# The recurrence's products of an mLSTM block as plain float32 matmuls instead of three float32r matmuls each

## The chip, the cores and the metric

The kernel runs on one core of a Trainium2 chip. The metric is the device time of one launch in microseconds (us). The engines are named as in the profile: PE is TensorE's matmul side and PEld its weight loads, DVE is VectorE, ACT is ScalarE, POOL is GpSimd, SP is the engine whose queue issues nearly all DMAs.

## The reference

The block takes x (2048 tokens x 1024 features, float32). It normalises x, projects it to four groups of 1024 columns, runs a pooling mixer on one half and a bidirectional mLSTM on the other, multiplies each by SiLU of its own z, and sends both through one output projection, a residual and a second norm. The change lies in the mLSTM alone. It has 4 heads of 256 features and 16 chunks of 128 tokens, and one scan per direction. Cut to what matters:

```
def step(carry, xs):                      # one chunk, one direction
    s   = (qj @ kj.T) * exp(log_D - m_t)                     # scores, weighted
    num = s @ vj + inter_w * (qj @ C)                        # chunk's values + state
    den = sum(s) + inter_w * (qj @ n)
    h   = num / max(|den|, exp(-m_t))
    C_new = decay * C + (ws * kj).T @ vj                     # update of the state
    n_new = decay * n + sum(ws * kj)
```

n is carried as a column beside C: the values end with a column of ones and a pad, so v has 258 columns.

## The kernel before, in words

Everything is float32 in memory, and nearly all large products are made of three float32r matmuls. A float32r operand is a float32 number whose low part is dropped; the kernel splits each operand into a high part (a cast on ScalarE) and a low part (the number minus its high part, on VectorE or GpSimd) and adds high x high, high x low and low x high in PSUM. The headwise maps (L336), the scores (L830) and the transposes are plain float32 matmuls already.

The order of the stages: input projections (`proj`, L135), the mLSTM's inputs (keys, values, convolved queries, written to DRAM), the gates, z of the first heads, the pooling mixer, then z of the last heads beside the 15 backward updates of head 0 (`next_backward`), and then the recurrence. It runs 64 steps (4 heads x 16 chunks). Step s computes both directions of its chunk from stored states: the forward state `cf` is carried on, the backward states `cb` of a head were made in the iterations of the head before it. What each iteration issues, in the order of every engine, is the table `order` (L991 to L1001): a piece, and by how many iterations it lags behind its step. In the first 53 iterations PE, DVE, ACT and POOL take exactly this order (`tc.manual_schedule`); for SP, and for all engines but PE later, a scheduler sets it.

One iteration has on PE: the forward `update` (two products of 128x128 weights by 258 columns), four units of the output projection (`fill`; a unit is three float32r matmuls of 512 columns, `po`, L704), `scores` of the next step, the backward `update`, two transposes `py`, a last part of units (`fill_rest`, on the mean 0.7 of one), and `numerators` (two products of scores by values and up to four of weighted queries by states). Around these, every operand is split: keys (`kh`, `kl`), values (`vh`, `vl`), states (`sh`, `sl`), weighted queries (`cwh`, `cwl`), weighted scores (`ph`, `pl`). The result `num` has one PSUM tile; VectorE makes the denominators from it (`denominators`), ScalarE and VectorE the ratios (`ratio0`, `ratio1`), which are its last readers. The updates' PSUM tile `upd` is also single, and VectorE adds it to the decayed state.

Small tiles in two buffers (pool `tp`) carry the pieces from one iteration to the next: `cw` (weighted queries, made by GpSimd two iterations ahead of their step), `dd` (weighted scores). The loaded keys `kk` have two buffers.

Of the kernel before, what the change touches and what calls it, by code (L numbers as in the profile page):

```python
# [10 lines left out]
F32 = mybir.dt.float32  # L11
F32R = mybir.dt.float32r
# [38 lines left out]
def hymba_block(ctx, tc, xT, x, w_in, wpxT, pool_w, bqT, bkT, bvT, bv, w_g, b_g, par, edge, w_out, g_out, out):  # L51
# [27 lines left out]
    # gate products that the recurrences use, token-major: column r = (dir, step, head)  # L79
# [16 lines left out]
    # ------------------------------------------------------------------ input projections  # L96
# [26 lines left out]
    # from the last z blocks on, TensorE runs in the order of the program  # L123
# [15 lines left out]
    # the small operands of the headwise maps, read ahead  # L139
# [3 lines left out]
    def load_headwise(i):  # L143
# [4 lines left out]
        # the map of q and, beside it, the gates' weights of k, q and v  # L148
# [12 lines left out]
    # W_poolx times the group's mix: pooling commutes with the mix of the channels  # L161
# [88 lines left out]
        # the array's clock rises while the first loads run  # L250
# [38 lines left out]
    # ---- the mLSTM's inputs  # L289
    with pm:  # L290
# [30 lines left out]
        def headwise(i, b):  # L321
# [3 lines left out]
            for src, off, rhs, dst in ((c, 0, mws[i], kk_s), (mxs[i], 2 + b * BT, hw[i]["vw"], v_s)):  # L325
                # v's columns end with ones, whose product with the keys is the denominator, and a pad
# [85 lines left out]
    # ---- z of the mLSTM (first heads) beside the gates: columns of gacc are (i|f, dir, head)  # L412
    with ExitStack() as pz:
# [31 lines left out]
        # in the order (dir, step, head)  # L445
# [15 lines left out]
        # rows r, columns t  # L461
# [34 lines left out]
        flat = lambda t: t.rearrange("p a b c -> p (a b c)")  # noqa: E731  # L496
# [30 lines left out]
    # ---- the pooling mixer  # L527
# [43 lines left out]
    # ------------------------------------------------------------------ mLSTM  # L571
# [21 lines left out]

    def keys_low(t):
        t["kl"] = t["pool"].tile([P, HD], F32R, name="kl")
        nc.vector.scalar_tensor_tensor(t["kl"], in0=t["k"], scalar=ws_tok[:, t["r"]:t["r"] + 1],  # L596
                                       in1=t["kh"].bitcast(F32), op0=ALU.mult, op1=ALU.subtract)

    def values_high(t):
        t["vh"] = t["pool"].tile([P, E], F32R, name="vh")  # L600
        nc.scalar.copy(t["vh"], t["v"])  # L601

    def values_low(t, eng=nc.gpsimd):
        t["vl"] = t["pool"].tile([P, E], F32R, name="vl")
        eng.tensor_tensor(t["vl"], t["v"], t["vh"].bitcast(F32), op=ALU.subtract)  # L605
# [20 lines left out]
    # the state that chunk j - 1 receives from its right  # L626
# [14 lines left out]
    def next_backward():  # L641
        if firsts:
# [3 lines left out]
            if "kh" not in bkv[f]:  # L646
                split_kv(bkv[f])
            backward(*f)
            if firsts and firsts[0] in bkv:
                split_kv(bkv[firsts[0]])  # L650

    # ---- the output projection: units of three products, and chores that go between them
# [67 lines left out]
    def fillers():  # L720
        # the first and the last tiles go in pairs by halves of the columns, while the other half's weights come
# [9 lines left out]
        def ahead(i):  # L731
            # reads y of piece i when it can be had
# [46 lines left out]
    # ---- a step of the forward direction, in pieces that go to different engines  # L779
# [20 lines left out]
    def mask(a):  # L800
        # keys s (partitions) that a query t may see: s <= t forward, s >= t backward
# [4 lines left out]
    # c times the weights of the states, and its parts  # L806
# [5 lines left out]

    def weighed_high(a):
        a["cwh"] = tp.tile([P, 2, 2, P], F32R, name="cwh")
        nc.scalar.copy(a["cwh"][:, a["ds"]], a["cw"][:, a["ds"]])  # L815

    def weighed_low(a, eng):
        ds = a["ds"]
        a["cwl"] = tp.tile([P, 2, 2, P], F32R, name="cwl")
        eng.tensor_tensor(a["cwl"][:, ds], a["cw"][:, ds], a["cwh"][:, ds].bitcast(F32), op=ALU.subtract)  # L820
# [284 lines left out]
```

## Time and profile before

| | |
|---|---|
| median of 3 runs | 1572.82 us (1572.33 to 1577.58) |
| profiled execution, first to last instruction | 1570.6 us |
| PE busy over the span | 1477.8 us (94%) |
| DVE / ACT / POOL busy | 1034.2 (66%) / 650.6 (41%) / 624.6 us (40%) |
| granted TensorE clock, mean | 0.992 of full speed |
| DMA | 231.25 MB, mean 147 GB/s |

The profiled execution lies 2.2 us under the median. A matmul's busy time reaches beyond the start of the next one, since matmuls are pipelined: what a matmul costs in a stream is the distance from its start to the next start. The recurrence lies between 857 us (first scores) and 1481 us (last scores); its iterations 0 to 52 end near 1325 us. After it only the rest of the output projection runs.

### The profile page before, as it was taken

The page shows a single profiled execution, that of the slowest core. Times are in us where ns is not written, and L with a number is a line of the kernel's source. Part 1 is how long each engine was busy: PE and PEld are TensorE (multiplying, and loading weights), DVE is VectorE, ACT ScalarE, POOL GpSimd, SP SyncE. Part 2 cuts the span into 40 slices and gives each one's busy share as a digit, 9 for nine tenths or more (in the row PEclk, how much of TensorE's full clock was granted, in tenths as well). Part 3 has the DMA queues.
Part 4 walks back from the last instruction along what each step waited for, and adds up shares of the span by engine and source line. Part 5 has one row for each costly group of instructions (what it writes and reads, how often), then busy time and mean ns, then how long its engine had stood idle before and what let it go on. Part 6 is the DMA issues. An engine that isn't in the chain of part 4 may idle for free.

```text
span 1570.6 us, 23151 instructions
## 1 busy us (share of the span) xinstructions
PE 1477.8 (94%) x7801; PEld 1257.9 (80%) x7801; DVE 1034.2 (66%) x1993; ACT 650.6 (41%) x1516; POOL 624.6 (40%) x752
## 2 busy tenths in 40 slices
PE   8899999999999999999999888888888899899998
PEld 6689888878888888888887777777777777787886
DVE  8795445562134333434543999999999999766753
ACT  6245443442011110001234666666666666635431
POOL 6543333310000222221020777777767778443300
PEclk9999999999999999999999999999999999999999
DMA  6268766542111101111337776676676667754352
GB/s 218 73 201 242 184 182 177 167 143 77 55 54 54 54 16 52 54 54 54 101 108 226 235 200 185 203 207 189 193 208 192 187 202 239 203 181 154 119 163 81
DMA packets 251351, 231.25 MB, mean 147 GB/s; under 512 B 18400, under 2 KB 211168, under 8 KB 250208
## 3 DMA queue, kind: packets, MB, share of 16 engines
q1 hardware_dynamic: 236768, 215.08, 45.9%
q10 hardware_dynamic: 14464, 14.68, 3.0%
q8 instruction: 62, 1.02, 0.3%
q14 instruction: 57, 0.47, 0.1%
HBM read 149.81 MB, written 79.89 MB: 146 GB/s over the span
## 4 chain that ended last, share of the span: by engine, by line
PE 56%; DVE 22%; DMA 8%; POOL 6%; issue 5%; ACT 3%; SPq 1%; POOLq 0%; DVEq 0%; ACTq 0%
PE proj L135 40%; PE po L704 7%; PE hw L336 4%; DVE yt L936 3%; DVE rstd L907 2%; DVE vl L605 2%; DMA gw<-g_s 2%; DVE cb L622 1%; DMA ym_s<-yt 1%; DVE yt L931 1%; PE hw L185 1%; DVE sl L869 1%; POOL cwl L820 1%; DVE kl L596 1%; POOL cw L810 1%
## 5 line engine op out<-in xcount | busy, mean ns | idle before, releaser
L135 PE MATMUL proj<-uh,whi 128*128 128x512 f32 x1024 | 403.8, 395 | 4.6 <-DVE mx L204 3.6
L135 PE MATMUL proj<-ul,whi 128*128 128x512 f32 x1024 | 401.5, 392 | 1.5 <-DVE ul L218 1.5
L135 PE MATMUL proj<-uh,wlo 128*128 128x512 f32 x1024 | 401.8, 393 | 0.4 <-DVE wlo L94 0.4
L135 PEld LDWEIGHTS proj<-uh,whi 128*128 128x128 f32 x1024 | 193.7, 189 | 43.3 <-DVE mx L204 3.7
L135 PEld LDWEIGHTS proj<-uh,wlo 128*128 128x128 f32 x1024 | 193.4, 189 | 41.7 <-DVE wlo L94 0.8
L135 PEld LDWEIGHTS proj<-ul,whi 128*128 128x128 f32 x1024 | 193.6, 189 | 40.9 <-DVE ul L218 2.6
L704 PE MATMUL po<-woh,yh 128*128 128x512 f32 x512 | 205.7, 402 | 3.2 <-DVE o L707 1.8
L704 PE MATMUL po<-woh,yl 128*128 128x512 f32 x512 | 202.4, 395 | 2.3 <-DVE yl L94 2.3
L704 PE MATMUL po<-wol,yh 128*128 128x512 f32 x512 | 202.0, 395 | 1.2 <-DVE wol L94 1.2
L91 ACT CAST whi<-wl 128x1024 fp32r<-128x1024 f32 x31 | 32.6, 1052 | 228.7 <-PE proj L135 225.5
L704 PEld LDWEIGHTS po<-woh,yl 128*128 128x128 f32 x512 | 96.6, 189 | 25.2 <-DVE yl L94 3.1
L616 PE MATMUL upd<-vh,kh 128*128 128x258 f32 x240 | 72.6, 302 | 46.8 <-ACT vh L601 45.1
L704 PEld LDWEIGHTS po<-woh,yh 128*128 128x128 f32 x512 | 96.7, 189 | 22.3 <-DVE o L707 2.4
L704 PEld LDWEIGHTS po<-wol,yh 128*128 128x128 f32 x512 | 96.8, 189 | 19.2 <-DVE wol L94 1.5
L316 DVE SCALAR_TENSOR_TENSOR c<-mx,par_sb,c 128x512 f32<-128x512 f32 x128 | 103.4, 825 | 3.0
L543 DVE TENSOR_TENSOR ux<-proj,rnorm 128x512 f32<-128x512 f32 x32 | 22.1, 691 | 124.7 <-PE proj L135 124.7
L869 POOL TENSOR_TENSOR sl<-cb,sh 128x516 fp32r<-128x516 f32 x60 | 86.5, 1441 | 29.9 <-ACT sh L864 25.4
L810 POOL TENSOR_TENSOR cw<-cT,gw 128x512 f32<-128x512 f32 (+1 forms) x64 | 91.8, 1434 | 7.8 <-DMA gw<-g_s 5.7
L556 POOL TENSOR_TENSOR win<-ux 128x2063 f32<-128x2063 f32 x8 | 29.0, 3624 | 160.7 <-DVE ux L543 160.7
L820 POOL TENSOR_TENSOR cwl<-cw,cwh 128x512 fp32r<-128x512 f32 (+1 forms) x64 | 90.3, 1411 | 6.4 <-ACT cwh L815 4.9
L616 PEld LDWEIGHTS upd<-vh,kh 128*128 128x128 f32 x240 | 45.2, 188 | 55.9 <-ACT hh L884 51.5
L843 POOL TENSOR_TENSOR pl<-dd,ph 128x256 fp32r<-128x256 f32 x64 | 51.4, 804 | 87.4 <-ACT ph L839 87.4
(216 smaller groups left out, 3187.4 us busy)
## 6 DMA issues: line engine op xcount, KB each, us to landing
gw<-g_s SPq DMA_DIRECT2D x128, 128.0 KB, 4.4
v<-v_s SPq DMA_DIRECT2D x124, 129.0 KB, 3.4
kk<-kk_s SPq DMA_DIRECT2D x124, 128.0 KB, 3.6
wl<-in_w_in SPq DMA_DIRECT2D x23, 512.0 KB, 3.9
xt<-in_xT SPq DMA_DIRECT2D x32, 256.0 KB, 4.1
cT_s<-c SPq DMA_DIRECT2D x32, 256.0 KB, 3.6
kk_s<-tokst SPq DMA_DIRECT2D x32, 256.0 KB, 2.6
kkT_s<-kkTb SPq DMA_DIRECT2D x32, 256.0 KB, 4.1
```

The costliest lines, as they stand in the source:

```text
L91: nc.scalar.copy(hi, src)
L135: pe(nc.tensor.matmul(ps, lhsT=l[:, kt, :], rhs=r[:, kt, :], start=(kt == 0 and n == 0), stop=(kt == KT - 1 and n == 2)))
L316: nc.vector.scalar_tensor_tensor(c, in0=mx[:, b * BT + t:(b + 1) * BT + t], scalar=par_sb[:, i, t:t + 1], in1=c, op0=ALU.mult, op1=ALU.add)
L336: nc.tensor.matmul(ps[:, e, :], lhsT=src[:, o:o + P], rhs=rhs, start=True, stop=True)
L605: eng.tensor_tensor(t["vl"], t["v"], t["vh"].bitcast(F32), op=ALU.subtract)
L616: pe(nc.tensor.matmul(ps[:, m, :E], lhsT=t[l][:, ms], rhs=t[r_], start=(n == 0), stop=(n == 2)))
L704: pe(nc.tensor.matmul(ps, lhsT=l[:, kt, :], rhs=r, start=(kt == 0 and e == 0), stop=(kt == 7 and e == 2)))
L810: eng.tensor_tensor(a["cw"][:, ds], a["cT"][:, None].broadcast_to([P, nd, 2, P]), a["gw"][:, 1, ds, None, :].broadcast_to([P, nd, 2, P]), ...
L820: eng.tensor_tensor(a["cwl"][:, ds], a["cw"][:, ds], a["cwh"][:, ds].bitcast(F32), op=ALU.subtract)
L843: eng.tensor_tensor(a["pl"], a["dd"], a["ph"].bitcast(F32), op=ALU.subtract)
L869: eng.tensor_tensor(a["sl", d], a["state", d], a["sh", d].bitcast(F32), op=ALU.subtract)
L936: eng.tensor_tensor(yt, yt, a["sz"], op=ALU.mult)
```

## The change

All products of the updates and numerators become one plain float32 matmul each, straight on the tiles that the parts were made from: `kw` (keys times the state weights, written as float32), `v`, `dd`, `cw` and the states `cf` and `cb`. The pieces that made parts, and their places in `order`, are gone. `v` gets a third buffer. The output projection and the input projections keep their three float32r matmuls. (The diff also drops comments; cut to its core here.)

```
-        v = pool.tile([P, E], F32, name="v", bufs=2)
+        v = pool.tile([P, E], F32, name="v", bufs=3)
-    def keys_high(t):
-        t["kh"] = t["pool"].tile([P, HD], F32R, name="kh")
-        nc.scalar.activation(t["kh"], t["k"], AF.Copy, scale=ws_tok[:, t["r"]:t["r"] + 1])
...
-    def keys_low(t):
...
-    def values_high(t):
...
-    def values_low(t, eng=nc.gpsimd):
...
-    def split_kv(t):
-        for piece in (keys_high, keys_low, values_high, values_low):
-            piece(t)
+    def weigh_keys(t):
+        t["kw"] = t["pool"].tile([P, HD], F32, name="kw")
+        nc.scalar.activation(t["kw"], t["k"], AF.Copy, scale=ws_tok[:, t["r"]:t["r"] + 1])
     def update(t, prev, pool, name, bufs):
...
-            for n, (l, r_) in enumerate((("kh", "vh"), ("kh", "vl"), ("kl", "vh"))):
-                pe(nc.tensor.matmul(ps[:, m, :E], lhsT=t[l][:, ms], rhs=t[r_], start=(n == 0), stop=(n == 2)))
+            pe(nc.tensor.matmul(ps[:, m, :E], lhsT=t["kw"][:, ms], rhs=t["v"], start=True, stop=True))
...
-    def weighed_high(a):
...
-    def weighed_low(a, eng):
...
-    def scores_high(a):
...
-    def scores_low(a, eng):
...
     def numerators(a):
...
-            for n, (l, r) in enumerate(((ph, kv["vh"]), (ph, kv["vl"]), (pl, kv["vh"]))):
-                pe(nc.tensor.matmul(num[:, d, :E], lhsT=l[:, d, :], rhs=r, start=(n == 0),
-                                    stop=(n == 2 and d not in a["dirs"])))
+            pe(nc.tensor.matmul(num[:, d, :E], lhsT=a["dd"][:, d, :], rhs=a["kv"]["v"], start=True,
+                                stop=d not in a["dirs"]))
         for d in a["dirs"][::-1]:
-            sh, sl = a["sh", d], a["sl", d]
+            state = cb.pop((a["h"], a["j"])) if d else a["cf"]
             for m in range(2):
-                for n, (l, r) in enumerate((("cwh", sh), ("cwh", sl), ("cwl", sh))):
-                    pe(nc.tensor.matmul(num[:, d, :E], lhsT=a[l][:, d, m, :], rhs=r[:, m, :],
-                                        start=False, stop=(m == 1 and n == 2)))
+                pe(nc.tensor.matmul(num[:, d, :E], lhsT=a["cw"][:, d, m, :], rhs=state[:, m, :],
+                                    start=False, stop=(m == 1)))
...
-    def state_high(a, d):
...
-    def state_low(a, d, eng):
...
     order = (
-        ("store", 3, V), ("scores_low", 0, G), ("denominators_2", 1), ("state_high_0", 0), ("ratio_0", 1),
-        ("forward", 0), ("back_values_high", -1), ("state_low_0", 0, V), ("ratio_1", 1), ("normalise_1", 2),
...
+        ("store", 3, V), ("denominators_2", 1), ("ratio_0", 1),
+        ("forward", 0), ("ratio_1", 1), ("normalise_1", 2),
+        ("fill", 0), ("fill", 0), ("moments_0", 1), ("fill", 0),
+        ("mask", -2), ("fill", 0), ("moments_1", 1), ("keys", -2),
+        ("scores", -1), ("moments_2", 1), ("backward", 0), ("transposes", 2), ("moments_3", 1),
         ("exponentials", -1), ("weigh", -2, G), ("normalise_0", 1), ("weigh_scores", -1), ("fill_rest", 0),
...
+        ("numerators", 0), ("back_keys", -1), ("join", 2), ("denominators_0", 0),
+        ("skip", 1), ("denominators_1", 0),
     )
```

What this does to the order on three engines, in the recurrence. PE before, from the end of a backward update (`upd`) over the transposes (`py`) and a unit of the output projection (`po`) to the first product of scores by values (`num`):

```order
L616 MATMUL upd<-vl,kh 128x258
L616 MATMUL upd<-vh,kl 128x258
L920 MATMUL py<-ident,hh 128x128 x2
L704 MATMUL po<-woh_6572,yh 128x512
L704 MATMUL po<-wol_6573,yh 128x512
L704 MATMUL po<-woh_6572,yl 128x512
L850 MATMUL num<-vh,ph 128x258
L850 MATMUL num<-vl,ph 128x258
L850 MATMUL num<-vh,pl 128x258
```

and the same place in the changed kernel:

```order
L597 MATMUL upd<-v,kw 128x258 x2
L869 MATMUL py<-ident,hh 128x128 x2
L685 MATMUL po<-woh_6422,yh 128x512
L685 MATMUL po<-wol_6423,yh 128x512
L685 MATMUL po<-woh_6422,yl 128x512
L812 MATMUL num<-v,dd 128x258 x2
L817 MATMUL num<-cb,cw 128x258 x2
L817 MATMUL num<-cf,cw 128x258 x2
```

A product was three rows (high by high, high by low, low by high) and is one; x2 stands for two products. The places in the iteration are the same.

GpSimd before, one iteration from the mask of the gate weights (`gw`) on, with what each instruction waits for besides its own engine's order:

```order
L803 AFFINE_SELECT gw<-gw 128x128 [waits DMAHW5_49]
L803 AFFINE_SELECT gw<-gw 128x128
L902 TENSOR_TENSOR rstd<-rstd,mhalf 128x1 [waits DVE_49]
L810 TENSOR_TENSOR cw<-cT,gw 128x512 [waits DMAHW6_49,DMAHW2_49,Pool_49]
L843 TENSOR_TENSOR pl<-dd,ph 128x256 [waits Activation_49]
L869 TENSOR_TENSOR sl_9609<-cb,sh_9564 128x516 [waits PE_49]
L820 TENSOR_TENSOR cwl<-cw,cwh 128x512
```

and after:

```order
L784 AFFINE_SELECT gw<-gw 128x128 [waits DMAHW2_49,Activation_49]
L784 AFFINE_SELECT gw<-gw 128x128
L851 TENSOR_TENSOR rstd<-rstd,mhalf 128x1 [waits DVE_49,Activation_49]
L791 TENSOR_TENSOR cw<-cT,gw 128x512 [waits DMAHW5_49,PE_49,Pool_49]
L784 AFFINE_SELECT gw<-gw 128x128 [waits DMAHW4_49,Activation_49]
```

Three of GpSimd's pieces (`pl`, `sl`, `cwl`) are gone. The weighted queries `cw` now wait for PE: their buffer was last read by GpSimd's `cwl` and ScalarE, and is now read by the numerators two steps back. Behind this wait stand the next mask and the next power (`rstd`).

VectorE before, from the backward state's evacuation (`cb`) to the reciprocal of the denominators (`rn`):

```order
L622 SCALAR_TENSOR_TENSOR cb<-cb,dec_bc,upd 128x516
L596 SCALAR_TENSOR_TENSOR kl<-kk,ws_tok,kh 128x256
L907 SCALAR_TENSOR_TENSOR rstd<-mv,rstd 128x1
L835 TENSOR_TENSOR dd<-dd,sT 128x256
L94 TENSOR_TENSOR yl<-y,yh 128x256
L596 SCALAR_TENSOR_TENSOR kl<-kk,ws_tok,kh 128x256
L931 SCALAR_TENSOR_TENSOR yt<-py,par_sb,yt 128x128 x2
L875 TENSOR_TENSOR rn<-num,em_tok 128x2
L605 TENSOR_TENSOR vl<-v,vh 128x258
L877 SCALAR_TENSOR_TENSOR rn<-num,rn 128x2
L936 TENSOR_TENSOR yt<-yt,sz 128x256
L880 RECIPROCAL rn<-rn 128x2
```

and after:

```order
L603 SCALAR_TENSOR_TENSOR cb<-cb,dec_bc,upd 128x516
L856 SCALAR_TENSOR_TENSOR rstd<-mv,rstd 128x1
L807 TENSOR_TENSOR dd<-dd,sT 128x256
L94 TENSOR_TENSOR yl<-y,yh 128x256
L880 SCALAR_TENSOR_TENSOR yt<-py,par_sb,yt 128x128 x2
L824 TENSOR_TENSOR rn<-num,em_tok 128x2
L826 SCALAR_TENSOR_TENSOR rn<-num,rn 128x2
L885 TENSOR_TENSOR yt<-yt,sz 128x256
L829 RECIPROCAL rn<-rn 128x2
```

Here two `kl` and one `vl` are gone (a `vl` and an `sl` more lie outside this piece); the rest keeps its order.

## Rows read from the trace of the kernel before

**Rows 1.** The page's head: the span of the profiled execution.
```profile
span 1570.6 us, 23151 instructions
```
**Rows 2.** Stretches (from:to us): length, busy us of engines (instructions), clock, DMA.
```profile
core 0: us, PE busy (x) PEld busy (x) DVE busy (x) ACT busy (x) POOL busy (x), PEclk, DMA share, GB/s
720.00:860.00 140.00, 140.00 (x665) 117.79 (x664) 58.23 (x77) 35.79 (x67) 23.21 (x21) 1.00 0.41 127
860.00:1325.00 465.00, 404.45 (x2499) 353.54 (x2498) 455.39 (x1047) 304.83 (x778) 334.65 (x363) 1.00 0.70 203
1325.00:1481.00 156.00, 148.45 (x764) 124.73 (x763) 115.47 (x271) 82.39 (x214) 68.71 (x78) 0.98 0.58 176
```
**Rows 3.** VectorE groups, 860 to 1325 us: xcount | busy us, mean ns | idle before.
```profile
L936 DVE TENSOR_TENSOR yt<-yt,sz 128x256 f32<-128x256 f32 x50 | 64.4, 1288 | 0.0
L596 DVE SCALAR_TENSOR_TENSOR kl<-kk,ws_tok,kh 128x256 fp32r<-128x256 f32 x97 | 55.6, 573 | 0.0
...
L869 DVE TENSOR_TENSOR sl<-cf,sh 128x516 fp32r<-128x516 f32 x48 | 49.9, 1039 | 0.0
L605 DVE TENSOR_TENSOR vl<-v,vh 128x258 fp32r<-128x258 f32 x97 | 46.8, 482 | 0.0
L622 DVE SCALAR_TENSOR_TENSOR cf<-cf,dec_bc,upd 128x516 f32<-128x516 f32 x45 | 32.7, 726 | 0.0
...
L880 DVE RECIPROCAL rn<-rn 128x2 f32<-128x2 f32 x51 | 7.8, 152 | 0.1
```
**Rows 4.** ScalarE group of the first ratio, same stretch.
```profile
L884 ACT ACTIVATE hh<-num,rn 128x256 f32<-128x256 f32 x51 | 24.2, 474 | 96.1 <-DVE rn L880 95.9
```
**Rows 5.** TensorE groups, same stretch.
```profile
L704 PE MATMUL po<-woh,yl 128*128 128x512 f32 x245 | 96.3, 393 | 0.0
...
L616 PE MATMUL upd<-vh,kh 128*128 128x258 f32 x188 | 57.8, 307 | 46.8 <-ACT vh L601 45.1 <-ACT woh L91 1.0 <-DVE cb L622 0.4
...
L856 PE MATMUL num<-sh,cwh 128*128 128x258 f32 x194 | 55.0, 283 | 0.0
...
L850 PE MATMUL num<-vh,ph 128*128 128x258 f32 x104 | 32.0, 308 | 2.4 <-DVE hh L888 0.7
L830 PE MATMUL sT<-cT,kkT 128*128 128x128 f32 x208 | 31.6, 274 | 1.4 <-DVE dd L835 1.4
...
L920 PE MATMUL py<-ident,hh 128*128 128x128 f32 x100 | 19.6, 277 | 5.1 <-ACT hh L910 5.1
```
**Rows 6.** TensorE timeline near 304 us: start us, us, line, tile, form, xcount.
```profile
303.82 1.14 PE L336 MATMUL hw<-mw,c 128*128 128x144 f32 x8
304.80 1.14 PE L336 MATMUL hw<-vw,mx 128*128 128x144 f32 x8
305.78 0.60 PE L344 MATMUL hw<-ident,tokst 128*128 128x128 f32 x4
```
**Rows 7.** TensorE timeline of one iteration of the recurrence, from 1199 us.
```profile
1199.17 0.28 PE L850 MATMUL num<-vl,ph 128*128 128x258 f32 x1
...
1201.12 0.28 PE L856 MATMUL num<-sh,cwl 128*128 128x258 f32 x1
...
1202.54 0.40 PE L704 MATMUL po<-wol,yh 128*128 128x512 f32 x1
...
1204.82 0.39 PE L704 MATMUL po<-woh,yl 128*128 128x512 f32 x1
1205.05 0.60 PE L830 MATMUL sT<-cT,kkT 128*128 128x128 f32 x4
```
**Rows 8.** TensorE groups over the whole span: the first record of each split product.
```profile
L616 PE MATMUL upd<-vh,kh 128*128 128x258 f32 x240 | 72.6, 302 | 46.8 <-ACT vh L601 45.1 <-ACT woh L91 1.0 <-DVE cb L622 0.4
...
L856 PE MATMUL num<-sh,cwh 128*128 128x258 f32 x240 | 68.3, 285 | 0.0
...
L850 PE MATMUL num<-vh,ph 128*128 128x258 f32 x128 | 39.1, 306 | 3.0 <-DVE hh L888 1.4
```
**Rows 9.** GpSimd group of the weighted queries, 860 to 1325 us.
```profile
L810 POOL TENSOR_TENSOR cw<-cT,gw 128x512 f32<-128x512 f32 x46 | 70.3, 1528 | 0.0
```

More of the change, by code (lines that the diff above doesn't have):

```diff
@@ L645, in next_backward @@
             f = firsts.pop(0)
-            if "kh" not in bkv[f]:
-                split_kv(bkv[f])
+            if "kw" not in bkv[f]:
+                weigh_keys(bkv[f])
             backward(*f)
             if firsts and firsts[0] in bkv:
-                split_kv(bkv[firsts[0]])
+                weigh_keys(bkv[firsts[0]])
     weights, wo, chores = {}, {}, []
@@ L811, in weigh @@
                           a["gw"][:, 1, ds, None, :].broadcast_to([P, nd, 2, P]), op=ALU.mult)
-    def weighed_high(a):
-        a["cwh"] = tp.tile([P, 2, 2, P], F32R, name="cwh")
-        nc.scalar.copy(a["cwh"][:, a["ds"]], a["cw"][:, a["ds"]])
-    def weighed_low(a, eng):
-        ds = a["ds"]
-        a["cwl"] = tp.tile([P, 2, 2, P], F32R, name="cwl")
-        eng.tensor_tensor(a["cwl"][:, ds], a["cw"][:, ds], a["cwh"][:, ds].bitcast(F32), op=ALU.subtract)
     def exponentials(a):
@@ L991, in hymba_block @@
     order = (
-        ("store", 3, V), ("scores_low", 0, G), ("denominators_2", 1), ("state_high_0", 0), ("ratio_0", 1),
-        ("forward", 0), ("back_values_high", -1), ("state_low_0", 0, V), ("ratio_1", 1), ("normalise_1", 2),
-        ("fill", 0), ("fill", 0), ("state_low_1", 0, G), ("moments_0", 1), ("weighed_low", 0, G), ("fill", 0),
-        ("mask", -2), ("fill", 0), ("values_high", -1), ("moments_1", 1), ("keys_high", -2), ("values_low", -1, V),
-        ("scores", -1), ("moments_2", 1), ("backward", 0), ("transposes", 2), ("moments_3", 1), ("keys_low", -1),
+        ("store", 3, V), ("denominators_2", 1), ("ratio_0", 1),
@@ L997, in hymba_block @@
+        ("forward", 0), ("ratio_1", 1), ("normalise_1", 2),
+        ("fill", 0), ("fill", 0), ("moments_0", 1), ("fill", 0),
+        ("mask", -2), ("fill", 0), ("moments_1", 1), ("keys", -2),
+        ("scores", -1), ("moments_2", 1), ("backward", 0), ("transposes", 2), ("moments_3", 1),
         ("exponentials", -1), ("weigh", -2, G), ("normalise_0", 1), ("weigh_scores", -1), ("fill_rest", 0),
-        ("numerators", 0), ("back_keys_high", -1), ("back_keys_low", -1), ("join", 2), ("denominators_0", 0),
@@ L999, in hymba_block @@
-        ("back_values_low", -1, V), ("skip", 1), ("denominators_1", 0), ("weighed_high", -1), ("state_high_1", -1),
-        ("scores_high", -1),
+        ("numerators", 0), ("back_keys", -1), ("join", 2), ("denominators_0", 0),
+        ("skip", 1), ("denominators_1", 0),
     )
     pieces = dict(
-        keys_high=lambda t: keys_high(t["kv"]), keys_low=lambda t: keys_low(t["kv"]),
-        values_high=lambda t: values_high(t["kv"]), values_low=lambda t, e: values_low(t["kv"], e),
-        mask=mask, weigh=weigh, weighed_high=weighed_high, weighed_low=weighed_low, exponentials=exponentials,
@@ L1006, in hymba_block @@
-        scores=scores, weigh_scores=weigh_scores, scores_high=scores_high, scores_low=scores_low,
+        keys=lambda t: weigh_keys(t["kv"]),
+        mask=mask, weigh=weigh, exponentials=exponentials, scores=scores, weigh_scores=weigh_scores,
         numerators=numerators, ratio_0=ratio0, ratio_1=ratio1, forward=forward, skip=skip,
         transposes=transpose_step, join=join, store=store_step)
-    for n, piece in (("state_high", state_high), ("state_low", state_low), ("denominators", denominators),
-                     ("moments", moments), ("normalise", normalise)):
+    for n, piece in (("denominators", denominators), ("moments", moments), ("normalise", normalise)):
@@ L1011, in hymba_block @@
         pieces.update({f"{n}_{k}": lambda t, *e, k=k, piece=piece: piece(t, k, *e) for k in range(4)})
-    backs = dict(back_keys_high=keys_high, back_keys_low=keys_low, back_values_high=values_high,
-                 back_values_low=values_low)
+    backs = dict(back_keys=weigh_keys)
     def run(span):
```

19 lines of the change are left out of this document (removed).

## The prediction

> **What bounds the kernel now.** I read the stretches first, then the groups of VectorE and TensorE inside the one that stood out, then TensorE's timeline for the distance from start to start. The profiled execution lasts 1570.6 us [rows 1], 2.2 us under the median of 1572.8; I sum against the execution and add the result to the median. In the stretch from 860 to 1325 us, which holds the first 53 iterations of the recurrence, VectorE is busy 455 of 465 us and TensorE 404; before it, from 720 to 860, TensorE has no idle time at all, and after it, from 1325 to 1481, it is busy 148 of 156 [rows 2]. So the recurrence's main stretch waits for VectorE and the rest for TensorE. The ratio on ScalarE shows the chain: it stood idle 95.9 us for VectorE's reciprocal [rows 4], and what ScalarE does behind it (the cast `vh`) is what TensorE's update waited for, 45.1 us [rows 5].
>
> TensorE's busy time counts the overlapping ends of matmuls, so I count starts. A float32r matmul of 258 columns takes 0.122 us (16 starts from 1199.17 to 1201.12), one of 512 takes 0.228 (10 starts from 1202.54 to 1204.82), a float32 record of 128 columns 0.109 (four records last 0.60, and one 0.274: three distances) [rows 5, 7]. In the stretch there are 3 x 245 `po`, 3 x (188 + 194 + 104) = 1458 records of 258 columns, 208 of the scores and 100 of the transposes [rows 5]. That is 167.6 + 177.9 + 22.7 + at most 10.9 = 379 us of needed stream in 465: 86 us in which TensorE could have worked and did not.
>
> **What is removed.** From VectorE's stretch go `kl` 55.6, `sl` 49.9 and `vl` 46.8 us [rows 3]: 152 of 455 leave 303. ScalarE loses six casts and GpSimd three pieces an iteration; neither was the bound. With 303 us VectorE would need 5.9 us an iteration where TensorE, below, needs over 8, so TensorE is late next and its own stream sets the pace.
>
> **What is added.** One product goes from three float32r matmuls, 3 x 0.122 = 0.366 us, to one float32 matmul, which the trace shows as two records (two products of scores a step, and four records). No float32 matmul of 258 columns is in the trace. The nearest rows are eight records of 144 columns in 0.98 us, 0.1225 each [rows 6], and the 0.109 at 128 columns. The line through them has 0.84 ns a column and gives 0.1225 + 114 x 0.00084 = 0.218 us a record, 0.436 a product; in proportion to 144 it would be 0.2195. From above I bound it by the float32r matmul of 512 columns, about twice 258, at 0.228 to 0.230: 0.460 a product. From below, if 114 more columns cost only what float32r columns do, (0.228 - 0.122) / 254 = 0.42 ns each, it is 0.170 a record and 0.340 a product, cheaper than now; the two float32 rows speak against it, since they already show twice that slope. I take 0.436: 0.070 more a product. The weight load of the second record lies beside the first record's stream, as in the eight records at 0.1225.
>
> There are 240 + 240 + 128 = 608 products [rows 8], 486 of them in the main stretch [rows 5], so 122 outside it. That is 34.0 us in the main stretch and 8.5 outside, 42.6 in all.
>
> The Trainium skill (FP8 and Floating Point Precision, TensorE Precision Notes) speaks against the change: true float32 takes four passes through the array, and the reduced form one, so four passes replace three. By this alone a product gains one pass of 258 columns, 0.1075 us at 2.4 GHz, 65 us over 608 products (an estimate), and the forecast below would be 22 us later. The rows agree that a float32 product costs four passes (two records of two), but the float32r pass costs 0.122 here and not 0.1075, so the sum goes by the rows.
>
> **The waits that change.** `cw` on GpSimd now waits for the numerators two steps back, so it starts only when an iteration's numerators are done. Queued behind it are the next mask and the power for the norm; `cw` takes 1.53 us [rows 9] and is needed a whole iteration later, so nothing waits. The load of `v` on SP's queue waits for the numerators of the step that had its buffer, since it is read there now and not by a cast earlier; that is what its third buffer is for, and it is wanted two iterations later. Behind it on the queue stand loads that are a whole iteration early too. The numerators wait for `dd`, `cw` and the states directly, all made at least an iteration before or, for `cf`, after the previous iteration's update. I cost these edits at nothing. The cover is TensorE's own 5 us between two numerators; without it each microsecond costs 51 us over the stretch.
>
> **The sum.** Main stretch: 379 + 34 = 413 us of stream, plus idle time that I let stand. Of the 86 us some never hung on the splits: the transposes' wait for `hh` 5.1, the scores' for `dd` 1.4 and the numerators' for `hh` 0.7 [rows 5], and the small steps where one form of matmul follows another, which I put at 0.2 us an iteration, 10 us. I take 18. So 431 us for 465: 34 saved. Outside: 8.5 dearer; 7.5 us of idle time stand between 1325 and 1481 [rows 2], of which I let half, 4, be filled, so 4.5 lost. Between 720 and 860, where TensorE has no idle time, the dearer updates are paid in full. 34 - 4.5 = 29.5 saved: 1570.6 - 29.5 = 1541.1 for the execution, 1543 for the median.
>
> **Rivals.**
> Dearer record: the float32 record costs 0.230, as a 512-column float32r one. 608 x 0.024 = 14.6 us more: 1558. For it: float32r columns of 512 are the only rows with as long a stream. Against: the rows of 144 columns.
>
> Cheaper record or a stretch with hardly any idle time: 5 us of idle for 18, and a record of 0.210, gives 13 + 9.7 off: 1520.
>
> Half of the idle time stays, as small waits of TensorE for other engines, 43 us for 18: 1568, within the noise. For it: the stretch has four engines in lockstep, and each wait removed uncovers another. Against: at 303 us VectorE has a third of the stretch free.
>
> Slower: the one `num` tile makes a loop that takes VectorE's place as the bound. From the end of the numerators to the last read of `num` come two denominator operations, the store's product (1.29, held up by GpSimd, and `cw` now starts at just this moment), the reciprocal (0.15, and the denominators taken as long), the first ratio 0.47, the forward state 0.73 and a second ratio of the first one's size [rows 3, 4]: 0.3 + 1.29 + 0.15 + 0.47 + 0.73 + 0.47 = 3.4 us. TensorE's other work between two numerators is four products of updates, 1.74, four units, 12 x 0.228 = 2.74, and scores and transposes, 0.6: 5.1 us. The loop decides from 5.1 us on; it has 1.7 to spare. If VectorE's queue and the lock add 3.1 and make it 6.5, TensorE idles 1.4 us more in each of 51 iterations, 71 us: 1614, slower than before. Against it is that VectorE is no longer full.
>
> **How the numbers follow.** Forecast 0.60 (its own range 1529 to 1553); dearer record 0.17; cheaper 0.08; half of the idle time stays 0.07; the loop 0.08. A measurement of this kernel tells about 0.5% from no change, 7.9 us, so faster means under 1565. The first three are faster: 0.85. The fourth is the same: 0.07. The loop is slower: 0.08. The range goes from 1523, near the cheaper case, to 1565, past the dearer one; it leaves out the loop, the half-idle case and part of the cheaper, under 2 in 10.
>
> **What would show it.** The profile after should have two records a product, 0.218 apart; the 53 iterations in about 431 us, some 8.1 us each; VectorE busy near 70% there, TensorE's wait for `vh` gone and no wait of over 10 us in total in its place; the stretch from 720 to 860 about 2 us longer. Records 0.23 apart show the dearer case. The prediction is wrong if TensorE waits at the numerators for a ratio, or if its idle time in the iterations stays above 40 us.

## The result and the profile after

The changed kernel takes 1521.05 us (median of 4 runs, 1520.67 to 1523.09), the kernel before, beside it, 1572.88. The ratio is 0.9666, 95% interval 0.9652 to 0.9680: faster by 52 us. The forecast was 1543 and the range began at 1523, so the direction was right and the gain 22 us larger than forecast. The profiled execution spans 1519.2 us, 51.4 less than before's [rows 1].

Three groups of rows tell where the time went. First the starts of the scores (`sT`) of step 0 and of step 53, which bound the main stretch; before, then after. The line gives the minimum, median and maximum of a record in ns, and the first and last start in us.

```profile
L830 PE MATMUL sT<-cT,kkT x4: 270/274/275, 857.5 to 857.8; 128*128 128x128 f32 x4
...
L830 PE MATMUL sT<-cT,kkT x4: 271/274/275, 1325.8 to 1326.1; 128*128 128x128 f32 x4
```

```profile
L802 PE MATMUL sT<-cT,kkT x4: 270/274/275, 859.0 to 859.4; 128*128 128x128 f32 x4
...
L802 PE MATMUL sT<-cT,kkT x4: 273/275/275, 1281.3 to 1281.6; 128*128 128x128 f32 x4
```

The stretch fell from 468.3 to 422.3 us. Split into needed stream (the count of each kind of record times its distance from start to start where nothing holds it up) and idle time, between the same starts:

| us | before | after |
|---|---|---|
| start of the recurrence | 857.5 | 859.0 |
| main stretch: needed + idle | 378.1 + 90.2 | 414.5 + 7.8 |
| scores 53 to scores 63 (the tail): needed + idle | 140.8 + 14.4 | 146.7 + 0.8 |
| from there to the last `po` | 82.2 | 83.0 |

The split hangs on the prices taken: with the median distance of every kind of record (0.232 us for a `po`) the main stretch is 383.5 + 84.9 us before and 418.1 + 4.1 after, so its parts are known to some 5 us, their changes to 2. The dearer products cost nearly what was foreseen (36.4 + 5.9 + 1.5 + 0.8 = 44.6 us for 42.6). The idle time that they met is nearly all gone.

The stretches of the profile after, the main stretch and the tail; columns as in [rows 2].

```profile
859.00:1281.00 422.00, 418.92 (x2029) 356.86 (x2029) 299.98 (x811) 183.46 (x484) 128.47 (x212) 1.00 0.79 228
1281.00:1429.00 148.00, 148.00 (x684) 123.69 (x683) 94.49 (x241) 59.65 (x164) 28.58 (x45) 1.00 0.61 184
```

VectorE went from 98% of its stretch to 71%, and TensorE from 87% to 99%. TensorE is now the bound in all of it.

TensorE's groups of the stretch, 862 to 1281 us, which answer to [rows 5]:

```profile
L685 PE MATMUL po<-woh,yh 128*128 128x512 f32 x245 | 109.0, 445 | 0.0
L597 PE MATMUL upd<-v,kw 128*128 128x258 f32 x376 | 97.4, 381 | 3.1 <-ACT hh L833 1.9 <-DVE cb L600 1.2
...
L812 PE MATMUL num<-v,dd 128*128 128x258 f32 x208 | 53.8, 381 | 0.0
L817 PE MATMUL num<-cb,cw 128*128 128x258 f32 x196 | 50.7, 381 | 0.0
L817 PE MATMUL num<-cf,cw 128*128 128x258 f32 x192 | 49.6, 380 | 0.0
```

Two records a product (376 for 188), and 3.1 us of waits where 46.8 stood at the first `upd` alone. The mean of 381 ns holds the overlapping end; the price is in the timeline of one iteration, which answers to [rows 7]:

```profile
1008.00 1.03 PE L817 MATMUL num<-cf,cw 128*128 128x258 f32 x4
1008.88 1.03 PE L597 MATMUL upd<-v,kw 128*128 128x258 f32 x4
1009.56 0.58 PE L685 MATMUL po<-woh,yh 128*128 128x512 f32 x1
1009.98 0.39 PE L685 MATMUL po<-wol,yh 128*128 128x512 f32 x1
...
1014.78 1.03 PE L812 MATMUL num<-v,dd 128*128 128x258 f32 x4
1015.65 1.03 PE L817 MATMUL num<-cb,cw 128*128 128x258 f32 x4
```

Four records take 0.87 us, 0.2175 each and 0.435 a product, and follow each other without a gap. From the four records of `upd` at 1008.88 to the second `po` at 1009.98 are 1.10 us, 4 x 0.2175 + 0.23: the change from one form of matmul to the other costs nothing.

VectorE's groups, same stretch, which answer to [rows 3], with the one-element operation of the norm (`rstd`), the reciprocal's input and GpSimd's `cw` [rows 9]:

```profile
L885 DVE TENSOR_TENSOR yt<-yt,sz 128x256 f32<-128x256 f32 x50 | 63.8, 1276 | 0.0
...
L856 DVE SCALAR_TENSOR_TENSOR rstd<-mv,rstd 128x1 f32<-128x1 f32 x51 | 8.9, 175 | 4.7 <-POOL rstd L851 4.4
...
L824 DVE TENSOR_TENSOR rn<-num,em_tok 128x2 f32<-128x2 f32 x52 | 8.3, 159 | 63.8 <-PE num L817 63.7
```

```profile
L791 POOL TENSOR_TENSOR cw<-cT,gw 128x512 f32<-128x512 f32 x46 | 59.2, 1288 | 129.9 <-issue 63.0 <-PE num L817 56.5 <-DMA gw<-g_s 7.5
```

VectorE now waits 63.7 us for the numerators where it made TensorE wait: the chain has turned round. `cw` waits 56.5 us for the numerators, and nobody waits for it. The store's product still takes 1276 ns; 48 of the 50 begin while a `cw` runs.

### The profile page after: what moved, and what is told of

It is laid out like the page before. It is cut to its first block, busy times and chain, and to the rows that moved or that the text cites. A ratio compares the mean times of both kernels' runs of the same rounds, so it can differ in the third digit from the quotient of the medians.

```text
span 1519.2 us, 21070 instructions
## 1 busy us (share of the span) xinstructions
PE 1493.2 (98%) x7193; PEld 1259.9 (83%) x7193; DVE 845.6 (56%) x1700; ACT 494.6 (33%) x1144; POOL 359.8 (24%) x549
## 4 chain that ended last, share of the span: by engine, by line
PE 91%; DVE 3%; DMA 3%; ACT 1%; POOL 1%; issue 1%; SPq 0%; DVEq 0%; POOLq 0%; ACTq 0%
PE proj L135 42%; PE po L685 23%; PE upd L597 7%; PE num L817 7%; PE hw L336 4%; PE num L812 4%; PE sT L802 2%; PE hw L185 1%; PE py L869 1%; DVE ul L218 1%; PE hw L344 1%; DVE c L316 1%; DMA kk<-kk_s 1%; DMA xt<-in_xT 1%; DMA wost<-in_w_out 1%
## 5 line engine op out<-in xcount | busy, mean ns | idle before, releaser
L685 PE MATMUL po<-woh,yh 128*128 128x512 f32 x512 | 217.6, 425 | 0.0
L597 PE MATMUL upd<-v,kw 128*128 128x258 f32 x480 | 124.2, 381 | 3.1 <-ACT hh L833 1.9
L791 POOL TENSOR_TENSOR cw<-cT,gw 128x512 f32<-128x512 f32 (+1 forms) x64 | 79.0, 1234 | 168.5 <-issue 77.9
L597 PEld LDWEIGHTS upd<-v,kw 128*128 128x128 f32 x480 | 87.3, 190 | 14.9 <-ACT hh L833 2.0
L784 POOL TENSOR_SCALAR_AFFINE_SELECT gw<-gw 128x128 f32<-128x128 f32 x128 | 43.8, 365 | 172.6 <-DMA gw<-g_s 170.5
L875 ACT ACTIVATE yt<-cT,par_sb 128x128 f32<-128x128 f32 x128 | 44.5, 394 | 108.8 <-DMA ym_s<-yt 108.7
L851 POOL TENSOR_TENSOR rstd<-rstd,mhalf 128x1 f32<-128x1 f32 x64 | 35.1, 549 | 174.5 <-DVE rstd L849 99.8
L833 ACT ACTIVATE hh<-num,rn 128x256 f32<-128x256 f32 x64 | 30.1, 471 | 141.9 <-DVE rn L829 133.8
```

The lines of the kernel that those rows point to most:

```text
L597: pe(nc.tensor.matmul(ps[:, m, :E], lhsT=t["kw"][:, ms], rhs=t["v"], start=True, stop=True))
L685: pe(nc.tensor.matmul(ps, lhsT=l[:, kt, :], rhs=r, start=(kt == 0 and e == 0), stop=(kt == 7 and e == 2)))
L784: nc.gpsimd.affine_select(out=a["gw"][:, 0, d, :], in_=a["gw"][:, 0, d, :], compare_op=ALU.is_ge, fill=BIG, base=0, pattern=[[pat, P]], ch ...
L791: eng.tensor_tensor(a["cw"][:, ds], a["cT"][:, None].broadcast_to([P, nd, 2, P]), a["gw"][:, 1, ds, None, :].broadcast_to([P, nd, 2, P]), ...
L851: nc.gpsimd.tensor_tensor(a["rstd"][:, 0:1], a["rstd"][:, 0:1], mhalf[:, :1], op=ALU.pow)
L875: nc.scalar.activation(a["yt"][:, m, :], a["cT"][:, m, :], AF.Copy, scale=par_sb[:, i, 8:9])
```

## The experiments

A ratio is to the kernel before on the same chip. Stretch, tail and idle time are counted as in the table above. "VectorE's work" is its busy share of 860 to 1280 us times the length of the main stretch; the kernel before has 459 us of it by [rows 2].

### Each half of the change alone, and the changed kernel again

e3 is the kernel before with the updates alone made plain, e4 with the numerators (scores by values, queries by states) alone; of the last two lines the first is e3's.

```
-            for n, (l, r_) in enumerate((("kh", "vh"), ("kh", "vl"), ("kl", "vh"))):
...
+            terms = (("kh", "vh"), ("kh", "vl"), ("kl", "vh")) if t["part"] else (("kh", "v"),)
+            for n, (l, r_) in enumerate(terms):
...
+FIRST, BACK, FWD, DV, ST = 0, 0, 0, 1, (1, 1)
+FIRST, BACK, FWD, DV, ST = 1, 1, 1, 0, (0, 0)
```

> The changed kernel itself, on the chip of the next three, as their yardstick: 0.967 of the kernel before.

> Half of the change: the updates (240 products) as plain float32 matmuls, the numerators (368) still as three float32r matmuls with their splits. Theory A: TensorE needs 418 - 298 x 0.073 = 396 us for iterations 0 to 52, VectorE 299 + sl 50 + half of vl 23 + collisions with GpSimd 45 = 417, so VectorE sets the pace again at 417 to 430: 1512 to 1528 us. If each half of the change gave its part of the gain by its number of products, 1573 - 52 x 240/608 = 1552 us.

> The other half: the numerators (368 products) as plain float32 matmuls, the updates (240) still split. Theory A: TensorE needs 418 - 188 x 0.073 = 404 us for iterations 0 to 52 and VectorE 299 + kl 56 + vl 47 = 402, so both are nearly full and wait for each other a little: 408 to 425 us, and 4 us less outside: 1505 to 1522 us. By its number of products it would be 1573 - 52 x 368/608 = 1541 us.

| | ratio (95%) | stretch: needed + idle | tail |
|---|---|---|---|
| e0, the changed kernel again | 0.9672 (0.9651 to 0.9693) | 414.5 + 8.5 | 147.5 |
| e3, updates | 0.9743 (0.9728 to 0.9759) | 392.3 + 38.2 | 153.1 |
| e4, numerators | 0.9701 (0.9668 to 0.9733) | 400.3 + 27.2 | 145.9 |

The halves win 2.6% and 3.0%, the whole 3.3%: they don't add. Both missed the stretch expected of a full VectorE, 430.4 us for 417 to 430 and 427.5 for 408 to 425, and their times (medians 1536.9 and 1527.7 us) lie between that theory's and the sum by number of products. Either half takes away most of the idle time, and what one half would still save, the other has saved already.

### Work put back on VectorE or GpSimd

The changed kernel with VectorE's (e1) or GpSimd's (e2) subtractions again, as work that nothing reads; e7 is e2 with that work in steps 0 to 52 alone. Of the edit, two pieces:

```
+    def idle_values(t, eng):
+        z = tp.tile([P, E], F32R, name="zv")
+        eng.tensor_tensor(z, t["v"], t["v"], op=ALU.subtract)
...
+    def idle_weighed(a, eng):
+        z = tp.tile([P, 2, 2, P], F32R, name="zc")
+        eng.tensor_tensor(z[:, a["ds"]], a["cw"][:, a["ds"]], a["cw"][:, a["ds"]], op=ALU.subtract)
```

> The changed kernel with VectorE's removed subtractions put back as work that nothing reads (two of 128x256 like kl, two of 128x258 like vl, one of 128x516 like sl in each iteration of the first 53, in their old places); GpSimd and ScalarE stay relieved. Theory A (VectorE's full queue made TensorE's idle time, and a plain product costs 0.07 us more than three float32r matmuls): VectorE again needs 299 + 152 = 451 us for iterations 0 to 52, so they take 455 to 465 us for 422, and the kernel 1550 to 1570 us. Theory B (the relief of GpSimd and ScalarE made the gain, through collisions with VectorE and the casts in front of the ratio): 1520 to 1530 us.

> The changed kernel with GpSimd's three removed subtractions an iteration (128x256, 128x516, 128x512) put back as work that nothing reads; VectorE and ScalarE stay relieved. Theory A: GpSimd rises to about 310 of 420 us and holds VectorE up by some 45 us (the one-element rstd at 1.0 for 0.17 us), VectorE needs about 345 of 420, TensorE still sets the pace: 1519 to 1527 us. Theory B: 1545 us and more.

> GpSimd's unread subtractions as in e2, but only for steps 0 to 52. e2 lost nothing there (423 us for 422) and 14 us after it, where weights of the second half are split on VectorE. Theory A (the loss lies where VectorE is full for a moment, at the change of halves): the loss goes, ratio 0.966 to 0.970, like the changed kernel's. If the loss came from the first 53 steps in another way (late loads handed on), it stays at 0.975.

Measured: e1 0.9861 (0.9828 to 0.9894), stretch 453.2 with 38.7 idle, tail 155.6. e2 0.9750 (0.9731 to 0.9769), stretch 422.8, tail 162.0. e7 0.9673 (0.9651 to 0.9695), stretch 423.6, tail 149.7. GpSimd's load alone costs nothing in the main stretch, and 14 us in the tail, for which e2's time missed both its ranges. e1's time came out in the range foreseen for a full VectorE, but not for that reason. Its busy times, 860 to 1280 us, and its waits:

```profile
860.00:1280.00 420.00, 396.86 (x1879) 332.77 (x1878) 337.69 (x976) 171.93 (x446) 118.13 (x191) 0.99 0.71 208
```

```profile
ACT kw L591 <- DMA kk<-kk_s: 120.5, 40, 5.5
...
DVE dd L831 <- ACT dd L797: 61.2, 34, 4.1
...
PE upd L597 <- ACT hh L857: 13.8, 13, 1.8
```

VectorE is 80% busy and itself waits 61.2 us, because ScalarE waits 120.5 us for the load of the keys `kk` before its exponentials `dd`. SP's queue in turn waits for the exponentials before a load of the gate weights `gw` (101.1 us, 39 times, 860 to 1310 us), with the load of `kk` behind it in order. By these rows the late keys make a loop over three engines. So e1 doesn't show a full VectorE, and the theory needed a kernel in which the loads have slack.

### The same with slack in the loads

e10 is the changed kernel with a third buffer for `kk` and for `yt`; e12 is e1 with it, e11 has both bodies of work and the buffers, e13 both bodies and the buffers as the change left them.

```
-        k = pool.tile([P, HD], F32, name="kk", bufs=2)
+        k = pool.tile([P, HD], F32, name="kk", bufs=3)
...
-        a["yt"] = tp.tile([P, 2, P], F32, name="yt")
+        a["yt"] = tp.tile([P, 2, P], F32, name="yt", bufs=3)
```

> The changed kernel with the same two buffers. TensorE sets its pace with 8 us of idle time in 422, so by every theory it gains at most that: ratio 0.963 to 0.968.

> The changed kernel with VectorE's subtractions as unread work, and a third buffer for kk and for yt. If the 31 us that VectorE's work cost without these buffers came by the loop of the key load, the keys and the exponentials (ScalarE waited 130 us for kk), the wait for kk goes and TensorE sets the pace again with VectorE at some 360 us: stretch 423 to 430, ratio 0.967 to 0.973. If VectorE's own queue made it, the stretch stays near 453 and the ratio near 0.986.

> The changed kernel with both bodies of unread work, VectorE's subtractions (zk, zv, zs0) and GpSimd's (zp, zc, zs1), and a third buffer for the keys kk and for yt, so that the loop of loads and keys that slowed the run with VectorE's work alone has slack. Theory A (a full VectorE made the idle time before): VectorE is busy 430 us and more of the stretch, TensorE idles 40 us or more there in waits for things that VectorE makes, stretch 455 to 475, ratio 0.985 to 1.005. Theory B (VectorE's load alone makes no idle time once the loads have a buffer; before, TensorE waited for the casts that ended the chain over the ratio): TensorE sets the pace, stretch 423 to 435, ratio 0.967 to 0.98 with some loss in the tail.

> The changed kernel with both bodies of unread work and the buffers as the change left them. Theory A: as before or slower, since TensorE's stream is also dearer: VectorE over 430 us busy, stretch 460 to 480, ratio 0.995 to 1.015. Theory B: as with VectorE's work alone, 453 in the stretch, and the tail 7 to 10 us longer: ratio 0.986 to 0.993.

| | ratio (95%) | VectorE's work | stretch: needed + idle | tail |
|---|---|---|---|---|
| e10, buffers | 0.9659 (0.9642 to 0.9676) | | 414.5 + 7.2 | 147.5 |
| e12, VectorE's work, buffers | 0.9669 (0.9653 to 0.9686) | 383 | 414.5 + 7.5 | 151.4 |
| e11, both, buffers | 0.9846 (0.9826 to 0.9866) | 415 | 414.5 + 19.0 | 167.5 |
| e13, both | 1.0013 (1.0000 to 1.0026) | 423 | 414.5 + 40.7 | 169.5 |

The busy times of e12, e11 and e13, each 860 to 1280 us, in this order:

```profile
860.00:1280.00 420.00, 417.18 (x2022) 356.38 (x2022) 381.45 (x1050) 176.84 (x481) 141.91 (x210) 1.00 0.78 227
```

```profile
860.00:1280.00 420.00, 407.64 (x1966) 346.14 (x1965) 402.53 (x1018) 172.49 (x469) 284.79 (x350) 1.00 0.76 221
```

```profile
860.00:1280.00 420.00, 392.91 (x1874) 331.62 (x1873) 390.50 (x974) 170.50 (x445) 266.12 (x332) 1.00 0.72 207
```

e12 settles that VectorE's queue alone didn't slow e1: with the buffers ScalarE's wait for `kk` fell to 0.4 us, and with VectorE at 91% TensorE sets the pace again. (The buffers of `kk` and of `yt` came together; which of them did it isn't told apart.) In e11 VectorE's work has grown to TensorE's needed stream (its operations last longer beside GpSimd's), and TensorE idles 11.5 us more. The stretch is what theory B gave, the ratio, because of 20 us in the tail, lies between the two. e13's time is theory A's: the whole gain is gone. But it isn't before's time over again: the tail is 14 us longer, and the stretch 13 shorter and near e1's 453.2, with the loads' loop in it, which the kernel before doesn't have. ScalarE's wait for the keys, 860 to 1280 us, before and in e13:

```profile
ACT kh L592 <- DMA kk<-kk_s: 0.2, 1, 0.2
```

```profile
ACT kw L591 <- DMA kk<-kk_s: 77.2, 39, 5.1
```

So e11 is the fairer measure of the subtractions: with slack in the loads they take back 11.7 us of the stretch and 20 of the tail, a little over half of the gain (0.9659 to 0.9846).

### Load taken off VectorE in the kernel before

Here TensorE's stream stays as before. e14 moves the store's product to GpSimd, e15 puts GpSimd's `cw` ahead of its power for the norm, e16 leaves VectorE's `vl` out.

```
-        ("store", 3, V), ("scores_low", 0, G), ("denominators_2", 1), ("state_high_0", 0), ("ratio_0", 1),
+        ("store", 3, G), ("scores_low", 0, G), ("denominators_2", 1), ("state_high_0", 0), ("ratio_0", 1),
...
-        ("mask", -2), ("fill", 0), ("values_high", -1), ("moments_1", 1), ("keys_high", -2), ("values_low", -1, V),
+        ("mask", -2), ("fill", 0), ("values_high", -1), ("moments_1", 1), ("weigh", -2, G), ("keys_high", -2), ("values_low", -1, V),
...
-        ("exponentials", -1), ("weigh", -2, G), ("normalise_0", 1), ("weigh_scores", -1), ("fill_rest", 0),
+        ("exponentials", -1), ("normalise_0", 1), ("weigh_scores", -1), ("fill_rest", 0),
...
     def values_low(t, eng=nc.gpsimd):
+        if eng is None:
+            t["vl"] = t["vh"]
+            return
```

> The kernel before, with the store's product (yt times sz, 1.29 us an iteration on VectorE) moved to GpSimd. TensorE's stream is as before. Theory A (VectorE, busy 455 of 465 us, sets the pace of before's main stretch): 50 to 64 us of work leave it, the stretch falls from 468 to 430-450, ratio 0.975 to 0.99. Theory B (the casts and subtractions as a chain of small waits keep TensorE idle, however full VectorE is): the stretch stays within 8 us of 468, ratio 0.995 to 1.005, or grows because GpSimd's pieces come later.

> The kernel before, with GpSimd's weighted queries cw ahead of its power for the norm instead of behind it, so that VectorE's one-element rstd operation (1043 ns there, 175 after the change) does not fall into cw. Theory A, and the long rstd is time that VectorE is held up by cw: rstd falls under 300 ns, VectorE is busy 30 to 45 us less, if no other operation is held up in its place; stretch 430 to 455, ratio 0.97 to 0.993. If cw only holds up another operation, or rstd now waits for the later power, VectorE's sum stays and so does the time: 0.995 to 1.005.

> The kernel before without VectorE's subtraction vl in the steps: the matmuls that read vl read vh instead (the values' low part is left out and the high part counted twice), so TensorE's stream is as before and VectorE has 47 us less. Theory A: the stretch falls by 30 to 47 us to 421-438, ratio 0.97 to 0.982. Theory B: what hangs on the split chain stays (TensorE's wait for vh of 45 us), the stretch falls by less than 15, ratio over 0.99.

| | ratio (95%) | VectorE's work | stretch: needed + idle |
|---|---|---|---|
| before | | 459 | 378.1 + 90.2 |
| e14, store on GpSimd | 0.9987 (0.9976 to 0.9998) | 440 | 378.1 + 86.5 |
| e15, `cw` earlier | 0.9899 (0.9883 to 0.9915) | 429 | 378.1 + 72.4 |
| e16, no `vl` | 0.9817 (0.9802 to 0.9832) | 414 | 378.1 + 62.8 |

e14's time is theory B's; e15's and e16's are theory A's, though e16's stretch is 3 us above its range. In this order the stretch falls with VectorE's work, by 4, 18 and 27 us for 19, 30 and 45. VectorE's load does pace the kernel before, but each microsecond taken off it gives back some 0.6 at best, for two reasons that the rows show. VectorE's groups in e16, 860 to 1280 us:

```profile
L596 DVE SCALAR_TENSOR_TENSOR kl<-kk,ws_tok,kh 128x256 fp32r<-128x256 f32 x95 | 83.3, 877 | 0.0
...
L94 DVE TENSOR_TENSOR yl<-y,yh 128x256 fp32r<-128x256 f32 x60 | 37.7, 646 | 2.7 <-ACT yh L91 2.7
...
L939 DVE TENSOR_TENSOR yt<-yt,sz 128x256 f32<-128x256 f32 x47 | 28.6, 608 | 0.0
```

`kl` took 573 ns before [rows 3] and takes 877 here, while the store fell from 1288 to 608: which operation GpSimd holds up is a matter of place, and the hold moves on. In e14 `yl` went from 444 to 903 ns, and only 19 of the 64 us that left VectorE stayed gone; and with the store's product on GpSimd, TensorE waited for `cwl` behind it, 860 to 1280 us:

```profile
PE num L856 <- POOL cwl L820: 22.5, 37, 1.0
PE upd L616 <- DVE kl L596: 8.6, 10, 1.0
```

### TensorE's stream as before, with no parts made

e6 gives each product three equal float32r matmuls on the high parts; of the pieces that made parts only ScalarE's cast of `v` stays. e8 is e6 with the third buffers for `kk` and `yt`.

```
-            pe(nc.tensor.matmul(ps[:, m, :E], lhsT=t["kw"][:, ms], rhs=t["v"], start=True, stop=True))
...
+            for n in range(3):
+                pe(nc.tensor.matmul(ps[:, m, :E], lhsT=t["kw"][:, ms], rhs=t["vh"], start=(n == 0), stop=(n == 2)))
```

> The changed kernel with three equal float32r matmuls of the high parts for each product, and no low parts: the operands are written as float32r by the instruction that makes them, and ScalarE rounds v. It leaves the low parts out and counts each product three times. TensorE's stream is that of the kernel before, the other engines are relieved. Theory A: TensorE is the only bound, so 608 x 0.073 = 44 us go: 1476 to 1488 us where the changed kernel has 1521, ratio 0.938 to 0.946. Theory C (DMAs, busy 0.79 in the stretch, or the chain from numerators to ratio set the pace just under TensorE's present one): 1505 us and more, ratio over 0.957.

> e6 (three equal float32r matmuls, low parts left out) with a third buffer for yt, whose free buffer ScalarE waited for behind the store's DMA (165 us in the first 53 steps of e6), and for kk. Theory D (the limit just under TensorE's pace is this wait: it holds ScalarE's next ratio back and so hh, which the transposes wait for): iterations 0 to 52 go from 409 to 390 us or less, ratio 0.942 or lower (e6 0.953). Theory C (the DMAs themselves, busy 0.80): no change, 0.951 to 0.955.

Measured: e6 0.9534 (0.9505 to 0.9563), stretch 408.9 with 30.7 idle, tail 145.0; e8 0.9502 (0.9477 to 0.9527), stretch 400.8, tail 150.0. e6 lies between its two theories. With the parts gone and the stream unchanged, 59.4 of the 90.2 us of idle time go. Among what stays are waits of a loop over the store's DMA, e6's largest of ScalarE and TensorE, 860 to 1265 us:

```profile
ACT yt L883 <- DMA ym_s<-yt: 160.7, 48, 7.0
PE py L877 <- ACT hh L867: 14.0, 11, 2.9
```

But the third buffers won only 8 of the 30.7 us, where 19 or more were expected of this loop, and in e8 ScalarE still waits 111.5 us for the store; what holds the rest is open. Against e6, the plain products cost 13.4 us in the stretch (408.9 to 422.3) and not 36.4: the changed kernel, with the longer stream, has 23 us less idle time.

### A mix of both forms

e5 keeps the updates of the first backward states, and up to step 52 the forward updates and the scores by values, as three float32r matmuls (`FIRST, BACK, FWD, DV, ST = 1, 0, 1, 1, (0, 0)`), with `vl` and `pl` on GpSimd. e9 is e5 with the third buffers.

> The changed kernel, but three float32r matmuls with their splits for the products whose splits have room: the first backward updates (30 products, where TensorE has no idle time), and up to step 52 the forward updates (100) and the products of scores by values (106), with the low parts of values and scores on GpSimd and only kl on VectorE. Theory A: TensorE, at its limit, is relieved of 236 x 0.073 = 17 us, and VectorE needs 299 + 30 + collisions 30 = 359 of some 405 us: 15 to 18 us under the changed kernel, ratio 0.955 to 0.959 to the kernel before. If VectorE's waits come back with any split: no gain, 0.965 to 0.97.

> e5 (splits kept where they have room) with the same two buffers; there ScalarE waited 99 us for keys (kk) and 57 us for yt. Theory D: iterations 0 to 52 go from 424 to 405 to 412 us, ratio 0.955 to 0.961 (e5 0.968). Theory C: 0.966 to 0.970.

Measured: e5 0.9679 (0.9654 to 0.9704), stretch 399.3 + 24.4; it won nothing over the change; ScalarE waited 98.5 us for `kk` and 46.7 for the store of `yt`. With both buffers, e9 0.9581 (0.9560 to 0.9602), 1511.3 us, stretch 399.3 + 9.5, tail 151.4: the fastest kernel here that computes the whole product, 0.8% under e10, the changed kernel with the same buffers. Its waits of TensorE, 860 to 1265 us, are short:

```profile
PE upd L628 <- ACT hh L917: 2.9, 1, 2.9
PE upd L628 <- DVE cb L632: 0.9, 1, 0.9
...
PE py L953 <- ACT hh L943: 0.7, 1, 0.7
```

## Why the prediction was wrong

**Right, by its own terms.** The record: 0.2175 us for 0.218, and so 36.4 us more stream in the stretch for the 34 forecast (the split takes the float32r record at 0.120 where the forecast took 0.122; by the medians it is 34.6). The Trainium skill's four passes (FP8 and Floating Point Precision, TensorE Precision Notes) agree: 0.435 us for two records of two passes, 0.109 a pass; but a float32r pass costs 0.121 here, so the change adds 0.072 a product and not a pass of 0.1075. The edits costed at nothing cost nothing that shows in the 7.8 us. The loop over `num` doesn't bind: VectorE waits 63.7 us for the numerators. VectorE is at 71% for the 70 named, `vh`'s wait is gone and nothing over 10 us is in its place. z's stretch grew by 1.5 us for 2.

**The step that failed** is the idle time that I let stand. In the main stretch it was 18 us, 7.2 from listed waits and 10 for the small steps where one form of matmul follows another, rounded up. The timeline shows these steps at no cost, and the stretch has 7.8 us of idle time in all. By the table, with before's idle time counted at 90.2, the stretch saved 46.0 where 34 were forecast: 12 of the 22 us. By the table 10.2 of these 12 are the idle time that I let stand; the rest lies in how the 86 us and the stream were counted, within the 5 us to which the split is known.

**The other 10 us** are the term of 7.5 us of idle time behind the main stretch, of which I let half be filled. 7.5 is a difference of busy times, and TensorE's busy time holds the overlapping ends, as the prediction itself said of the main stretch. Counted by starts the tail had 14.4 us, and 13.6 of them were filled. So the part outside the main stretch gained 5.4 us instead of losing 4.5. The runs point at GpSimd's subtractions as the largest part of what was filled: put back beside the plain products they make the tail 14 us longer (e2), left out of the tail 2 (e7), and VectorE's make it 4 to 8 us longer (e12, e1). Before took 155.2 us there, e3, which keeps GpSimd's three pieces, 153.1, and e4 without them 145.9.

The cheaper rival, 1520 us, came closest, with its 5 us of idle time, but by luck: its record of 0.210 was wrong, and with the record as measured it would have said 1530; the tail, which it left alone, made up for that. It was given 0.08.

**The cause, tested.** That the main stretch waits for VectorE was right in direction and too simple. e6 shows the making of the parts as a whole: without it, but for one cast, and with TensorE's stream as before, 59.4 of the 90.2 us of idle time go. e16 and e15 show that VectorE's load paced the kernel before. TensorE's wait for ScalarE's cast `vh`, the largest that is listed, was mostly VectorE's lateness handed on: it nearly goes in e16, where ScalarE still makes all its casts and the update waits for VectorE's `kl` instead. Before, then e16 (two lines), 860 to 1280 us:

```profile
PE upd L616 <- ACT vh L601: 43.9, 39, 1.7
```

```profile
PE upd L619 <- DVE kl L596: 16.7, 24, 0.9
...
PE upd L619 <- ACT vh L601: 3.5, 8, 1.3
```

e12 shows that the same subtractions on VectorE cost the changed kernel next to nothing in the main stretch once the loads have slack, e11 that those of both engines together do cost time. But before's idle time was no single queue's: part of VectorE's time was GpSimd holding it up, and when VectorE is relieved, the loads of `kk` (e1, e5), the store of `yt` (e6) and GpSimd's chain (e14) are next. That it vanished all together is best explained by the change taking work off three engines and lengthening TensorE's stream at the same time. How the 62.8 us that are left in e16 divide among these isn't settled, and no run put ScalarE's casts back: what share they have is open.

## What to carry to other kernels

Where TensorE waits for the work that prepares its operands, a dearer matmul that needs no preparation can win: price the matmul at start-to-start distance, and the work removed on every other engine. What is left idle afterwards is read wait by wait, and with no allowance for steps that the timeline doesn't show; idle time is counted by starts in every stretch, not by busy time. And when one engine's load is lifted, look at the loops through loads and buffers next: a third buffer did nothing for the changed kernel (e10) and was worth 1% to the mix (e5 to e9).

## What the runs showed of the hardware

The one-element `rstd` took 1043 ns on the mean of the main stretch before, 860 to 1325 us, and 175 after:

```profile
L907 DVE SCALAR_TENSOR_TENSOR rstd<-mv,rstd 128x1 f32<-128x1 f32 x51 | 53.2, 1043 | 2.9 <-POOL rstd L902 2.9
```

Both engines' timelines of the kernel before show why, VectorE first, then GpSimd:

```profile
1201.59 1.27 DVE L907 SCALAR_TENSOR_TENSOR rstd<-mv,rstd 128x1 f32<-128x1 f32 x1
```

```profile
1201.22 1.63 POOL L810 TENSOR_TENSOR cw<-cT,gw 128x512 f32<-128x512 f32 x1
```

It ends at 1202.86, with GpSimd's `cw` (1202.85); 43 of the 51 begin while a `cw` runs and end within 0.1 us of its end. The Trainium skill (SBUF — State Buffer, SBUF: two separate sides) says that the two engines share a pair of ports, taken for a whole instruction by whichever starts first, where VectorE's operation has two inputs in SBUF; the two rows agree. With `cw` moved, e15's rows, 860 to 1280 us, show who is held instead:

```profile
L94 DVE TENSOR_TENSOR yl<-y,yh 128x256 fp32r<-128x256 f32 x56 | 36.8, 674 | 2.3 <-ACT yh L91 2.3
L907 DVE SCALAR_TENSOR_TENSOR rstd<-mv,rstd 128x1 f32<-128x1 f32 x47 | 7.1, 150 | 7.8 <-POOL rstd L902 7.8
```

`rstd` is at 150 ns, and `yl`, 444 ns in the kernel before and 417 in the changed one, at 674. I had expected neither that the change would free this time, since GpSimd's `cw` now starts later, nor that 44 us of VectorE's busy time before were such a hold (51 times 1043 less 175).
